# Three-block weight sums of the output projection, made in SBUF from the two-block sums instead of in memory beside the attention heads

## The chip, the cores and the metric

One core of one Trainium2 chip runs the whole program. A time is the device time of one execution in microseconds (us). Where a comparison of two kernels is given, it is of executions on the same chip.

The engines named here are PE (matrix multiply; PEld is its weight load), DVE, ACT and POOL (element-wise work), SP (in this kernel it only issues DMAs), and the core's 16 DMA engines. DMAs are issued by two queues for the most part: SP's (q1 in the profile) and POOL's (q0). Only those of POOL can add what they move to what stands at the destination.

## The reference, cut to what matters

Two layers, each with one input projection, three groups of attention heads, gates, and one output projection, in float32:

```python
h = jnp.einsum('bsd,dn->bsn', x, w_in)            # 512 x 2048 by 2048 x 8278
y_fox = fox_attention(...)                         # 6 heads, 512 keys, forget bias
y_dsa = dsa_attention(...)                         # 6 heads, rotary, 128 selected keys
y_mem = memory_attention(...)                      # 4 heads on 256 memory tokens
y = jnp.concatenate([y_fox, y_dsa, y_mem], axis=-1)   # each times silu(gate)
y = jnp.einsum('bsn,nd->bsd', y, w_out)            # 512 x 2048 by 2048 x 2048
return layer_norm(ALPHA * x + y, ln_gain, ln_bias)
```

## The kernel before

**Precision.** Every float32 product is made of three matrix products: both operands are split into a high and a low part, and high*high, high*low and low*high are added up. The split of a weight tile is one ACT instruction (the high part, `whi`) and one DVE instruction (the low part, `wlo`).

**Stages of a layer.** The index projections; the "values" and "second" stages, in which most columns of the input projection are made; the heads, beside whose steps eight remaining head columns are projected (PE work `c<-...`); and the output projection ("out", PE work `z<-...`). `now[1]` holds the stage's name while the program is written.

**The output projection as seven products.** The 2048 x 2048 product is cut into blocks in the way of Strassen and Winograd, so that seven products of quarter size do the work of eight. `PRODUCTS` names them. Some take sums of weight blocks for their right side: T1 is block (0,0) plus (0,1); T3 is (0,1) plus (1,1); T2, with three blocks, is T1 plus (1,1), or T3 plus (0,0); T4 is T2 plus (1,0). `OUT_ORDER` gives the order, each product for two pairs of column blocks: P1, P1, P7, P7, Q6, Q6, Q4, Q4, Q5, Q5, P2, Q3, P2, Q3. P7 takes T3, Q6 takes T2, Q4 takes T4 and Q5 takes T1.

**Halves.** Each of these 14 steps takes two weight chunks of 1 MB, and each chunk comes in two halves of 512 KB (128 x 1024). A half is 12 matmuls of 512 columns (two row blocks, two 512-column parts, three products). There are 56 halves; they are numbered from 0 here, so that P1 is 0 to 7, P7 8 to 15, Q6 16 to 23, Q4 24 to 31, Q5 32 to 39.

**What is issued beside half n.** The loop at the end of the program does, for each half n: `grow_w(n + 2)`, then `load_w` for the chunk two ahead (half n + 4), then `split_w(n + 3)`, then the matmuls of half n. So a half is loaded four halves ahead and split three ahead. After the last half of a step, `residual` adds the product from PSUM to the tiles `z`, which `load_res` fetched through POOL's queue: two tiles at the start of each of steps 2 to 5 (`RES_LOADS`), four at steps 0 and 1.

**Sums in memory.** `weight_sums` makes a sum of weight blocks in DRAM: first a DMA copies one block (1 MB) into a new DRAM tile `sum`, later a second one adds another block to it. `all_sums` is a generator that is stepped between chunks, and `paced` sets how often: not in the stages "kv" and "second", at each step beside the heads, every third step in "out". Outside "values", `pool_waits` stands ahead of each of these DMAs: a DVE copy `mark` and a POOL instruction `seen` that reads it, so that POOL comes to the DMA no earlier than DVE to that place. Of the output projection's sums there are four of each kind in a layer (two pairs, two chunks): T3, T1 and T2.

**Sums in SBUF.** A chunk of the kind "grown" isn't loaded. `grow_w` adds one more block, by POOL's DMA, to the raw weights of an earlier product, as soon as these have been split; the tile is then the raw weights of the later one. Q4's T4 is grown in this way from Q6's T2. `load_w` puts the weights that another will be grown from into small tiles `grown` (128 x 512 out of the pool `slots`) and all others into tiles `raw` (128 x 1024 out of a pool of seven, which the heads use too).

**Heads.** What a head needs is fetched by SP from memory: transposed columns (`load_turned`, a DMA transpose `vraw<-vt`), values (`vraw<-v`), and for half of them a row of forget sums (`ck<-crow`), from which POOL makes the bias `bt`. POOL also makes the low part of the values, `vl`, which the head's last product `po` on PE takes. All queues are worked off in order: an SP that can't get rid of one DMA holds back all later ones.

Of the kernel before, what the change touches and what calls it, by code (L numbers as in the profile page):

```python
# [102 lines left out]
GROWN = {"Q6": ("P7", (0, 0)), "Q4": ("Q6", (1, 0))}  # L103
# [17 lines left out]
def all_chunks():  # L121

    out = []
    for l in range(DEPTH):
        out += [("mv", l, 0, g) for g in range(4)]
        out += [("mk", l, j, j * HD) for j in range(H_MEM)]
        out += layer_chunks(l)
    return out


def stream():

    wall = all_chunks()
    where = {c: i for i, c in enumerate(wall)}
    out = []

    def product(kind, l, name, pair, gs=(0, 1)):
        right = PRODUCTS[name][2]
        for g in gs:
            at = lambda step: where[kind, l, 2 * pair + step[1], 2 * step[0] + g]  # L140
            if name in GROWN and (kind == "val" or name == "Q4"):
                of, step = GROWN[name]
                src = ("grown", (of, at(step)))
            elif kind == "val" and right in PAIRED and pair >= IN_DRAM:
                src = ("pair", tuple(at(step) for step in PAIRED[right]))
            elif isinstance(right, str):
                src = ("sum", (kind, l, right, pair, g))
            else:
                src = ("wall", at(right))
            out.append(({"val": "vs"}.get(kind, kind), l, (name, pair), g, src))  # L150

    for i, c in enumerate(wall):
        kind, l, j = c[:3]
        if kind == "out":
            if c == ("out", l, 0, 0):
                for name, pair in OUT_ORDER:
                    product("out", l, name, pair)
        elif kind == "val":
            if c == ("val", l, 0, 0):
                for order in (VAL_FIRST, VAL_SECOND):  # L160
                    for pair in range(PAIRS):
                        for name, g in order:
                            product("val", l, name, pair, (g,))
        else:
            out.append((*c, ("wall", i)))
    return out
# [81 lines left out]
def kernel(  # L248
# [26 lines left out]
    def uid(name):  # L275
        count[0] += 1
        return f"{name}_{count[0]}"
# [3 lines left out]
    def slot(name, dt=F32, w=512):  # L281
        t = slots.tile([P, w], dt, tag="s", name=uid(name))
        if name in COUNTED:
            out_now.append(t)
        return t
# [35 lines left out]
    chunks = stream()  # L321
    raw, parts = {}, {}
    sums = {}
# [14 lines left out]
    def half(src, h):  # L338
        return src[:, h * H:(h + 1) * H]

    def load_w(i, pieces=2, some=(0, 1)):
        if i < len(chunks) and chunks[i][4][0] != "grown":
            kind, key = chunks[i][4]
            src = {"wall": lambda: wall[key], "sum": lambda: sums[key],
                   "pair": lambda: wall[key[0]]}[kind]()
            if chunks[i][0] == "out" and chunks[i][2][0] == "Q6":
                for h in some:
                    t = [slot("grown") for _ in range(2)]
                    raw.setdefault(i, []).append(t)
                    for c in range(2):  # L350
                        nc.sync.dma_start(t[c], half(src, h)[:, c * 512:(c + 1) * 512])
                return
            w = DM // pieces
            for c in range(pieces):
                if c * 2 // pieces not in some:
                    continue
                if c * 2 % pieces == 0:
                    raw.setdefault(i, []).append(raws.tile([P, H], F32, tag="raw", name=uid("raw")))
                nc.sync.dma_start(raw[i][-1][:, c * w % H:c * w % H + w], src[:, c * w:(c + 1) * w])
                if i < 3 and c * 2 % pieces == 0:  # L360
                    load_mem(2 * i + c * 2 // pieces)
                if kind == "pair":
                    for e in (2 * c, 2 * c + 1):
                        t = others[i, e] = slot("other")
                        nc.sync.dma_start(t, wall[key[1]][:, e * 512:(e + 1) * 512])
# [93 lines left out]
    def load_mem(j):  # L459
        mem_raw[j] = slot("memraw")  # L460
        eng = nc.scalar if j < 2 and not memT else nc.sync
        eng.dma_start(mem_raw[j], memt_in[:, j * 512:(j + 1) * 512])
# [15 lines left out]
    def split_x(k):  # L478
# [4 lines left out]
        first_sum(k, x)  # L483

    load_w(0, 4, (0,))
    load_w(0, 2, (1,))
    load_w(1, 2)
    load_w(2, 2)
    load_mem(6)
# [33 lines left out]
    def pool_waits():  # L523

        mark, seen = small("mark", 1), small("seen", 1)
        nc.vector.tensor_copy(mark, mhalf)
        nc.gpsimd.tensor_tensor(seen, mark, mhalf, op=ALU.mult)

    SUM_STEPS = {"T1": ((0, 0), (0, 1)), "T3": ((0, 1), (1, 1)), "T2": ("T1", (1, 1)),
                 "T4": ("T2", (1, 0))}  # L530

    def block(kind, l, pair, g, step):
        return wall[where[kind, l, 2 * pair + step[1], 2 * step[0] + g]]

    def add_weights(key, src):
        nc.gpsimd.dma_start(sums[key], src, accum_op=ALU.add, max_dma_last_dim=4 * DM)

    def weight_sums(kind, l, names, pairs, some=(0, 1)):

        for name in names:  # L540
            for n in some:
                step = SUM_STEPS[name][n]
                for pair in pairs:
                    for g in range(2):
                        key = (kind, l, name, pair, g)
                        if isinstance(step, str):
                            src = sums[kind, l, step, pair, g]
                        else:
                            src = block(kind, l, pair, g, step)
                        if now[1] != "values":  # L550
                            pool_waits()
                        if n:
                            add_weights(key, src)
                        else:
                            sums[key] = dram.tile([P, DM], F32, name=uid("sum"))
                            nc.gpsimd.dma_start(sums[key], src)
                        yield

    def paced(gen, steps=PACE):

        n = 0
        for _ in gen:
            n += 1
            while now[1] in ("kv", "second"):
                yield 1
            yield {"heads": 1, "out": 3, "index": 1 + n % 2}.get(now[1], steps)

    def value_sums(l):

        for name in ("T3", "T1"):  # L570
            for n in range(2):
                yield from weight_sums("val", l, (name,), range(IN_DRAM), (n,))

    def all_sums():


        for l in range(DEPTH):
            yield from paced(value_sums(l))
            yield from paced(weight_sums("out", l, ("T3", "T1", "T2"), range(2)))
            while l + 1 < DEPTH and now[0] == l:  # L580
                yield 1

# [10 lines left out]
    now = (0, "index")  # L593
# [932 lines left out]
    for i, (kind, l, j, col, _) in enumerate(chunks):  # L1526
        late = last_half(i)
        if kind == "out":
            step = OUT_ORDER.index(j)
            name, pair = j  # L1530
# [11 lines left out]
        elif kind == "vs":  # L1542
            name, pair = j
# [15 lines left out]
        for h in range(2):  # L1559
            n = 2 * i + h  # L1560
# [83 lines left out]
            if h == 0:  # L1644
                if (kind, j) in HEAD_CHUNKS:
                    if kind == "fq" and j == EARLY:
                        now = (l, "heads")
# [49 lines left out]
        if kind == "mv" and l > 0:  # L1697
            now = (l, "kv")
        if kind == "small":
            now = (l, "index")  # L1700
            stored.clear()
            heads_done.clear()
            memT.clear()
            left.clear()
            if l == 0:
                begin(all_sums(), whole=True)
        if kind == "vs":
            now = (l, "second" if name in ("Q5", "Q3") else "values")
# [13 lines left out]
        if kind == "out" and step == col == 0:  # L1722
            now = (l, "out")
# [4 lines left out]
        if kind == "fq" and j == EARLY:  # L1728
            now = (l, "heads")
# [93 lines left out]
```

## Time and profile before

| what | us |
|---|---|
| median of three runs | 1951.85 (1947.03 to 1957.21) |
| profiled execution | 1972.85 |
| its span, first to last instruction | 1970.8 |
| PE busy in it | 1871.0 (95%) |
| DVE busy | 1599.0 (81%) |
| ACT busy | 1084.7 (55%) |
| POOL busy | 395.0 (20%) |
| head projections `c` of the first layer, start of the first to start of the last | 618.4 to 768.7 |
| the same of the second layer | 1588.3 to 1763.8 |

The profiled execution took 21 us longer than the median of the others; all rows below are from it. Times inside it count from its first instruction. "PEclk" in a row is the share of full clock that PE was granted in the stretch; "DMA" is the mean share that the packets of the 16 DMA engines took, which comes out over 1 where packets of several queues overlap. A row `out<-in` names a written and a read tile. A row that counts instructions may lack a few.

### The profile page before, as it was taken

To read this page: it belongs to the slowest core of one execution; us is meant where nothing else is said; L and a number is where in the kernel's file an instruction comes from. 1 tells how busy PE (TensorE), PEld (TensorE's weight loads), DVE (VectorE), ACT (ScalarE), POOL (GpSimd) and SP (SyncE) were. 2 spreads that over 40 slices of the span, in tenths; PEclk is the share of its full clock that TensorE was granted. 3 is DMA by queue.
4 is the path that set the end of the run, shared out by engine and by line. 5 is a ranking of instruction groups with operands and counts; after the bars stand their busy time and mean duration, and the time that the engine had idled before them with its cause. 6 is when DMAs were issued, how large, how long until landed. Compare 5 with 4: busy or idle time off the path is not lost.

```text
span 1970.8 us, 26414 instructions
## 1 busy us (share of the span) xinstructions
PE 1871.0 (95%) x8930; PEld 1584.2 (80%) x8930; DVE 1599.0 (81%) x2575; ACT 1084.7 (55%) x1666; POOL 395.0 (20%) x571
## 2 busy tenths in 40 slices
PE   9999999999999997899999999999999899748997
PEld 8998888888878876788899888878887788637876
DVE  6789888999777876889968889989886677648798
ACT  5776445555556655655667745445554466337543
POOL 0112111112114131130201122112211042211311
PEclk9999999999999998999999999999999999879999
DMA  9885989889999998596678789998999999996975
GB/s 347 297 261 155 273 248 267 267 270 335 318 342 293 197 238 164 165 275 210 221 264 243 214 273 297 277 282 257 297 354 323 299 269 215 149 114 181 284 218 139
DMA packets 237796, 497.26 MB, mean 252 GB/s; under 512 B 94544, under 2 KB 110928, under 8 KB 232796
## 3 DMA queue, kind: packets, MB, share of 16 engines
q1 hardware_dynamic: 198780, 329.85, 55.8%
q0 software_dynamic: 38304, 164.68, 33.4%
q8 instruction: 70, 1.15, 0.2%
q10 hardware_dynamic: 576, 1.05, 0.1%
q14 instruction: 66, 0.54, 0.1%
HBM read 423.12 MB, written 122.71 MB: 277 GB/s over the span
## 4 chain that ended last, share of the span: by engine, by line
PE 62%; DMA 16%; DVE 10%; issue 6%; ACT 3%; SPq 2%; POOL 1%; DVEq 0%; POOLq 0%; ACTq 0%
PE v L232 33%; PE c L232 14%; PE z L232 8%; DMA other<-in_wall_dram 5%; DMA ck<-crow 3%; DVE wlo L232 3%; DMA vraw<-vt 3%; DMA raw<-in_wall_dram 3%; PE po L232 2%; DVE rope L232 2%; PE ix L232 2%; PE s L232 2%; SPq L1304 1%; DVE z L232 1%; DMA z<-x 1%
## 5 line engine op out<-in xcount | busy, mean ns | idle before, releaser
L232 ACT ACTIVATE whi<-raw 128x1024 fp32r<-128x1024 f32 (+1 forms) x513 | 539.4, 1055 | 469.0 <-PE v L232 240.8
L232 DVE TENSOR_TENSOR wlo<-raw,whi 128x1024 fp32r<-128x1024 f32 (+1 forms) x513 | 626.4, 1227 | 157.3 <-ACT whi L232 154.8
L232 PE MATMUL v<-whi,vxh 128*128 128x512 f32 x768 | 301.6, 393 | 7.9 <-DVE vraw L232 7.9
L232 PE MATMUL v<-wlo,vxh 128*128 128x512 f32 x768 | 300.4, 391 | 2.7 <-DVE wlo L232 2.7
L232 PE MATMUL v<-whi,vxl 128*128 128x512 f32 x768 | 300.2, 391 | 0.0
L232 PE MATMUL v<-whi,xh 128*128 128x512 f32 x576 | 224.2, 389 | 0.0
L232 PE MATMUL v<-whi,xl 128*128 128x512 f32 x576 | 224.1, 389 | 0.0
L232 PE MATMUL v<-wlo,xh 128*128 128x512 f32 x576 | 224.1, 389 | 0.0
L232 PE MATMUL c<-xh,whi 128*128 128x512 f32 (+1 forms) x544 | 202.1, 371 | 0.0
L232 PE MATMUL c<-xh,wlo 128*128 128x512 f32 (+1 forms) x544 | 199.4, 367 | 0.0
L232 PE MATMUL c<-xl,whi 128*128 128x512 f32 (+1 forms) x544 | 199.1, 366 | 0.0
L232 PE MATMUL z<-whi,yl 128*128 128x512 f32 (+1 forms) x434 | 169.9, 392 | 11.2 <-DVE yl L232 11.1
L232 PEld LDWEIGHTS v<-whi,vxh 128*128 128x128 f32 x768 | 145.2, 189 | 40.0 <-issue 10.3
L232 PE MATMUL z<-wlo,yh 128*128 128x512 f32 (+1 forms) x434 | 169.5, 391 | 2.9 <-DVE wlo L232 2.8
L232 PEld LDWEIGHTS v<-wlo,vxh 128*128 128x128 f32 x768 | 145.1, 189 | 33.2 <-DVE wlo L232 3.5
L232 PE MATMUL z<-whi,yh 128*128 128x512 f32 (+1 forms) x434 | 170.1, 392 | 1.4 <-ACT yh L232 1.4
L232 PEld LDWEIGHTS v<-whi,vxl 128*128 128x128 f32 x768 | 144.9, 189 | 30.5
L232 DVE TENSOR_TENSOR raw<-raw,other 128x512 f32<-128x512 f32 x160 | 104.6, 687 | 28.7 <-DMA other<-in_wall_dram 28.2
L232 PEld LDWEIGHTS v<-whi,xl 128*128 128x128 f32 x576 | 108.1, 188 | 22.6
L232 PEld LDWEIGHTS v<-wlo,xh 128*128 128x128 f32 x576 | 108.1, 188 | 22.5
L232 PEld LDWEIGHTS v<-whi,xh 128*128 128x128 f32 x576 | 108.1, 188 | 22.4
L232 PEld LDWEIGHTS c<-xh,wlo 128*128 128x128 f32 x544 | 102.8, 189 | 12.1
(199 smaller groups left out, 3352.5 us busy)
## 6 DMA issues: line engine op xcount, KB each, us to landing
raw<-in_wall_dram SPq DMA_DIRECT2D x371, 512.0 KB, 7.3
other<-in_wall_dram SPq DMA_DIRECT2D x160, 256.0 KB, 9.0
sum<-in_wall_dram POOLq DMA_DIRECT2D x32, 1024.0 KB, 12.1
raw<-in_wall_dram POOLq DMA_DIRECT2D x56, 512.0 KB, 8.2
raw<-sum SPq DMA_DIRECT2D x48, 512.0 KB, 6.0
v<-vraw POOLq DMA_DIRECT2D x72, 256.0 KB, 7.0
vt<-halves POOLq DMA_DIRECT2D x72, 256.0 KB, 6.5
vraw<-v SPq DMA_DIRECT2D x48, 256.0 KB, 5.8
```

The source lines that it names most:

```text
L232: return f(*args, **kw)
L1304: nc.sync.dma_start_transpose(t.bitcast(U16).rearrange("p (a r) -> p a r", a=1), vt_d[j][c])
```

## The change

Three things, and what follows from them:

- `GROWN` is now followed for all products of both kinds. So Q6's T2 is no longer loaded from a sum in memory: it is grown in SBUF out of P7's T3, by adding block (0,0), and Q4's T4 out of it as before. The same tiles serve P7, Q6 and Q4, so the small `grown` tiles are now filled for P7.
- T2 is no longer summed in memory: four copies of 1 MB from `sum` to `sum` and four additions of 1 MB are gone from each layer.
- `paced` doesn't step beside the heads. The four additions that complete T1 now come in "out".

For each layer, 16 DMAs of 256 KB that loaded T2 through SP are gone, and 16 additions of 256 KB through POOL come instead.

```diff
--- before.py
+++ after.py
@@ -138,7 +138,7 @@
         right = PRODUCTS[name][2]
         for g in gs:
             at = lambda step: where[kind, l, 2 * pair + step[1], 2 * step[0] + g]
-            if name in GROWN and (kind == "val" or name == "Q4"):
+            if name in GROWN:
                 of, step = GROWN[name]
                 src = ("grown", (of, at(step)))
             elif kind == "val" and right in PAIRED and pair >= IN_DRAM:
@@ -343,7 +343,7 @@
             kind, key = chunks[i][4]
             src = {"wall": lambda: wall[key], "sum": lambda: sums[key],
                    "pair": lambda: wall[key[0]]}[kind]()
-            if chunks[i][0] == "out" and chunks[i][2][0] == "Q6":
+            if chunks[i][0] == "out" and chunks[i][2][0] == "P7":
                 for h in some:
                     t = [slot("grown") for _ in range(2)]
                     raw.setdefault(i, []).append(t)
@@ -526,8 +526,7 @@
         nc.vector.tensor_copy(mark, mhalf)
         nc.gpsimd.tensor_tensor(seen, mark, mhalf, op=ALU.mult)
 
-    SUM_STEPS = {"T1": ((0, 0), (0, 1)), "T3": ((0, 1), (1, 1)), "T2": ("T1", (1, 1)),
-                 "T4": ("T2", (1, 0))}
+    SUM_STEPS = {"T1": ((0, 0), (0, 1)), "T3": ((0, 1), (1, 1))}
 
     def block(kind, l, pair, g, step):
         return wall[where[kind, l, 2 * pair + step[1], 2 * step[0] + g]]
@@ -543,10 +542,7 @@
                 for pair in pairs:
                     for g in range(2):
                         key = (kind, l, name, pair, g)
-                        if isinstance(step, str):
-                            src = sums[kind, l, step, pair, g]
-                        else:
-                            src = block(kind, l, pair, g, step)
+                        src = block(kind, l, pair, g, step)
                         if now[1] != "values":
                             pool_waits()
                         if n:
@@ -561,9 +557,9 @@
         n = 0
         for _ in gen:
             n += 1
-            while now[1] in ("kv", "second"):
+            while now[1] in ("kv", "second", "heads"):
                 yield 1
-            yield {"heads": 1, "out": 3, "index": 1 + n % 2}.get(now[1], steps)
+            yield {"out": 3, "index": 1 + n % 2}.get(now[1], steps)
 
     def value_sums(l):
 
@@ -576,7 +572,7 @@
 
         for l in range(DEPTH):
             yield from paced(value_sums(l))
-            yield from paced(weight_sums("out", l, ("T3", "T1", "T2"), range(2)))
+            yield from paced(weight_sums("out", l, ("T3", "T1"), range(2)))
             while l + 1 < DEPTH and now[0] == l:
                 yield 1
```

Where POOL's instructions stand is told by the built programs. In the rows below a number behind a name tells one buffer from another, `sum_3669`, `sum_4015`, `sum_4395` and `sum_4798` are the first layer's T1, and `vl` and `bt` belong to the heads.

POOL beside the heads of the first layer, before:

```order
L232 TENSOR_TENSOR seen_6085<-mark_6084,mhalf 128x1
L232 DMA sum_3669<-in_wall_dram 128x2048
L232 TENSOR_TENSOR vl_6082<-vraw_5921,vh_6081 128x512
L232 TENSOR_TENSOR seen_6158<-mark_6157,mhalf 128x1
L232 DMA sum_4015<-in_wall_dram 128x2048
L232 TENSOR_TENSOR vl_6178<-vraw_5944,vh_6177 128x512
L232 TENSOR_TENSOR seen_6285<-mark_6284,mhalf 128x1
L232 DMA sum_4395<-in_wall_dram 128x2048
L232 TENSOR_TENSOR seen_6377<-mark_6376,mhalf 128x1
L232 DMA sum_4798<-in_wall_dram 128x2048
L232 TENSOR_TENSOR seen_6427<-mark_6426,mhalf 128x1
L232 DMA sum_6430<-sum_3669 16x16384
```

And now, from the row ahead of the same `vl_6082`:

```order
L232 AFFINE_SELECT bt_6059<-bt_6059 128x128
L232 TENSOR_TENSOR vl_6082<-vraw_5921,vh_6081 128x512
L232 TENSOR_TENSOR vl_6168<-vraw_5944,vh_6167 128x512
L232 TENSOR_TENSOR vl_6473<-vraw_6207,vh_6472 128x512
L232 TENSOR_SCALAR bt_6556<-ck_6446,cq_1434 128x128
L232 AFFINE_SELECT bt_6556<-bt_6556 128x128
L232 TENSOR_SCALAR bt_6557<-ck_6446,cq_1434 128x256
```

No DMA of a sum, and no `seen`, stands between the heads' instructions any more; the second layer's rows differ in the same way.

POOL at the start of the first layer's output projection, before, ahead of the first growth (`vl_7907` and `vl_7999` are the last two heads' values):

```order
L232 DMA z_7959<-in_x_dram 128x512
L232 DMA z_7961<-in_x_dram 128x512
L232 TENSOR_TENSOR vl_7907<-vraw_7756,vh_7906 128x512
L232 TENSOR_TENSOR vl_7999<-vraw_7763,vh_7998 128x512
L232 DMA z_8076<-in_x_dram 128x512
L232 DMA z_8078<-in_x_dram 128x512
L232 DMA grown_8080<-in_wall_dram 128x512
L232 DMA grown_8081<-in_wall_dram 128x512
```

And now (`vl_7855` and `vl_7970` are those two heads' values; `grown_7754` and the three behind it are of halves 8 and 9):

```order
L232 DMA grown_7754<-in_wall_dram 128x512
L232 DMA grown_7755<-in_wall_dram 128x512
L232 DMA grown_7797<-in_wall_dram 128x512
L232 DMA grown_7798<-in_wall_dram 128x512
L232 TENSOR_TENSOR seen_7910<-mark_7909,mhalf 128x1
L232 DMA sum_3669<-in_wall_dram 128x2048
L232 DMA z_7918<-in_x_dram 128x512
L232 DMA z_7920<-in_x_dram 128x512
L232 DMA grown_7825<-in_wall_dram 128x512
L232 DMA grown_7826<-in_wall_dram 128x512
L232 TENSOR_TENSOR vl_7855<-vraw_7692,vh_7854 128x512
L232 DMA grown_7864<-in_wall_dram 128x512
```

The growth of P7's halves, an addition to T1 and two `z` loads now stand ahead of the values of the last two heads.

POOL later in the same stage, before, at the two `z` loads of step 5 (`z_8340`, `z_8342`):

```order
L232 DMA grown_8149<-in_wall_dram 128x512
L232 DMA grown_8150<-in_wall_dram 128x512
L232 DMA grown_8193<-in_wall_dram 128x512
L232 DMA grown_8194<-in_wall_dram 128x512
L232 DMA grown_8229<-in_wall_dram 128x512
L232 DMA grown_8230<-in_wall_dram 128x512
L232 DMA grown_8254<-in_wall_dram 128x512
L232 DMA grown_8255<-in_wall_dram 128x512
L232 DMA z_8340<-in_x_dram 128x512
L232 DMA z_8342<-in_x_dram 128x512
L232 DMA grown_8282<-in_wall_dram 128x512
L232 DMA grown_8283<-in_wall_dram 128x512
```

And now (`z_8307`, `z_8309`, which the residual behind half 23 takes):

```order
L232 DMA grown_7825<-in_wall_dram 128x512
L232 DMA grown_7826<-in_wall_dram 128x512
L232 DMA grown_7864<-in_wall_dram 128x512
L232 DMA grown_7865<-in_wall_dram 128x512
L232 DMA grown_7924<-in_wall_dram 128x512
L232 DMA grown_7925<-in_wall_dram 128x512
L232 DMA grown_7949<-in_wall_dram 128x512
L232 DMA grown_7950<-in_wall_dram 128x512
L232 TENSOR_TENSOR seen_8299<-mark_8298,mhalf 128x1
L232 DMA sum_4395<-in_wall_dram 128x2048
L232 DMA z_8307<-in_x_dram 128x512
L232 DMA z_8309<-in_x_dram 128x512
```

These two loads stood behind twelve pieces of growth, those of halves 16 to 21; now 28 pieces (halves 8 to 21) and three additions to T1 are ahead of them in the stage.

## The prediction

> **What bounds the kernel now.** The page first. PE is busy nearly all the time, so only places where it stands still can give anything back, and the chain that ended last says what they wait for.
>
> ```profile
> PE 1871.0 (95%) x8930; PEld 1584.2 (80%) x8930; DVE 1599.0 (81%) x2575; ACT 1084.7 (55%) x1666; POOL 395.0 (20%) x571
> PE 62%; DMA 16%; DVE 10%; issue 6%; ACT 3%; SPq 2%; POOL 1%; DVEq 0%; POOLq 0%; ACTq 0%
> ```
>
> Next the table of stretches (length, then busy time and count for PE, PEld, DVE, ACT, POOL; granted clock, DMA share, GB/s). The first two rows run from the first head projection to half 15 of the output projection, in layer 0 and in layer 1; the others are pieces of them.
>
> ```profile
> 618.00:847.00 229.00, 207.09 (x1026) 174.66 (x1025) 180.01 (x354) 138.05 (x298) 60.15 (x89) 0.95 0.92 206
> 1588.00:1841.00 253.00, 206.18 (x1025) 174.10 (x1025) 179.27 (x354) 137.63 (x298) 61.05 (x89) 0.91 0.94 187
> 740.00:760.00 20.00, 12.48 (x58) 10.38 (x58) 10.49 (x17) 6.01 (x11) 4.53 (x9) 0.85 1.18 163
> 760.00:780.00 20.00, 17.40 (x76) 14.93 (x76) 13.16 (x35) 14.66 (x35) 1.44 (x2) 0.76 0.54 131
> 1720.00:1740.00 20.00, 7.00 (x27) 5.54 (x27) 6.96 (x11) 5.25 (x10) 0.00 (x0) 0.67 1.19 73
> 1740.00:1760.00 20.00, 5.66 (x26) 5.30 (x27) 5.63 (x12) 4.71 (x8) 4.53 (x9) 0.56 1.13 206
> ```
>
> The same work takes 229 us in one layer and 253 in the other, with PE idle for 22 and 47 us. In the bad stretches DMA is over-full (1.13 to 1.19) and yet moves little in one of them (73 GB/s). The waits (who waited for whom; us in total, times, longest) in 1690 to 1770, and the last one in 600 to 840:
>
> ```profile
> POOL bt L232 <- DMA ck<-crow: 44.0, 1, 44.0
> PE po L232 <- POOL vl L232: 24.3, 1, 24.3
> PE pt L232 <- ACT bt L232: 9.0, 1, 9.0
> PE po L232 <- POOL vl L232: 8.7, 2, 7.5
> ```
>
> PE waits for `vl`, which stands behind `bt` on POOL, which waits for the row `ck`. Why `ck` is late is seen in time order (start, length, engine):
>
> ```profile
> 1683.30 0.88 POOL L232 DMA_DIRECT2D sum<-in_wall_dram  x1
> ...
> 1690.90 0.82 POOL L232 DMA_DIRECT2D sum<-in_wall_dram  x1
> ...
> 1696.82 0.80 POOL L232 DMA_DIRECT2D sum<-in_wall_dram  x1
> ...
> 1704.38 0.81 POOL L232 DMA_DIRECT2D sum<-in_wall_dram  x1
> 1690.32 42.82 SPq L1304 DMA_TRANSPOSE vraw<-vt  x2
> 1733.24 1.79 SPq L881 DMA_DIRECT2D ck<-crow  x1
> ```
>
> POOL issues the four additions that end T2; two transposes then hold SP for 42.8 us, and `ck` is issued after them. The DMA view of 1683 to 1750 (median us to landing last; queue q0 with packets, MB and share of the 16 engines) and, last line, the landings of `vraw` in 755 to 800, when no sum is under way:
>
> ```profile
> q0 software_dynamic: 576, 4.19, 40.1%
> sum<-in_wall_dram POOLq DMA_DIRECT2D x4, 1024.0 KB, 44.2
> vraw<-vt SPq DMA_TRANSPOSE x5, 25.2
> DMA to landing us min/median/max: 3.4/4.0/7.1
> ```
>
> 4 us for a transpose alone, 25 beside the additions. The Trainium skill ("DMA: Bandwidth & Descriptors", Queues, rings and completion order) says that a DMA engine takes turns among its queues, a whole packet of one, then of the next; the trace agrees in that many small packets of q1 wait behind fewer large ones of q0.
>
> **What the change takes away: the stalls beside the heads.** All twelve DMAs of sums leave that stage in each layer (four additions to T1 are moved, eight DMAs for T2 are gone). I count as theirs: in layer 1 the waits of 24.3 and 9.0 us, in layer 0 that of 8.7. Behind a stall PE runs at half clock for a while: 0.76 granted in 760:780 is 9.6 us at half, less the idle time in it; I take 4.8 us lost in layer 0, and 3.4 in layer 1, where most of the slow clock falls on idle time (0.67 and 0.56 above). Layer 0: 8.7 + 4.8 = 13.5. Layer 1: 24.3 + 9.0 + 3.4 = 36.7. Together 50.2 us. The other idle time up to half 15 (some 13 us a layer: short waits for DVE, the step into "out") stays. `mark` and `seen` cost nothing: POOL is busy 60 of 229 us.
>
> **What it adds: DMA work in "out".** The pace there, and the DMA queues in it: the first line is the end of the stage, the second the stretch from half 6 to half 24 (`z` alone; 18 halves of 12); then 840 to 885, where growth runs, with its queues and issues; then q1 alone in 900 to 960; then q0 in 1624 to 1637, which holds one addition into memory and a few packets.
>
> ```profile
> 900.00:920.00 20.00, 20.00 (x90) 16.54 (x89) 17.27 (x26) 9.86 (x11) 0.00 (x0) 1.00 0.65 216
> 816.00:872.00 56.00, 50.70 (x219) 40.26 (x218) 6.30 (x10) 0.00 (x0) 4.57 (x6) 1.00 0.80 224
> q0 software_dynamic: 2624, 5.24, 57.3%
> q1 hardware_dynamic: 2784, 6.63, 41.5%
> grown<-in_wall_dram POOLq DMA_DIRECT2D x16, 256.0 KB, 11.8
> z<-in_x_dram POOLq DMA_DIRECT2D x4, 256.0 KB, 12.5
> q1 hardware_dynamic: 3421, 12.19, 61.6%
> q0 software_dynamic: 144, 1.05, 44.2%
> ```
>
> 90 matmuls in 20 us are 2.67 us a half. Plain loads cost 61.6% of 60 us for 12.19 MB: 3.03 us per MB, so 0.79 for a tile `z` and 1.59 for a half. In 840 to 885 q0 and q1 add up to 98.8%: the DMA engines are full, and their work adds. q0 took 57.3% of 45 = 25.8 us; less four `z` (3.2) that is 22.6 for 16 pieces of growth, **1.41 us each**. One addition into memory: 44.2% of 13 = **5.75 us**.
>
> Before, the engines had 16 pieces of growth to do there, and PE did not stop. Now the first growth is issued behind half 6, and the `z` tiles of step 5, which the residual behind half 23 takes, stand behind 28 pieces and three sums. Work ahead of them: 28 x 1.41 = 39.5; 3 x 5.75 = 17.3; eight `z` 6.3; P7's last six halves by SP 9.5; together 72.6 us. Time for it: 56 us (second line), and a cushion: splits run three halves ahead, 8.0 us, less one half's split, 1.06 on ACT and 1.23 on DVE (the page's two rows below), so 5.7.
>
> ```profile
> L232 ACT ACTIVATE whi<-raw 128x1024 fp32r<-128x1024 f32 (+1 forms) x513 | 539.4, 1055 | 469.0 <-PE v L232 240.8
> L232 DVE TENSOR_TENSOR wlo<-raw,whi 128x1024 fp32r<-128x1024 f32 (+1 forms) x513 | 626.4, 1227 | 157.3 <-ACT whi L232 154.8
> ```
>
> What is late is 72.6 - 56 - 5.7 = 10.9 us; DVE then waits for `z`, the splits behind it wait, and PE stops. Growth of halves 22 and 23 follows and is late by no more, since the halt gives it time. In layer 1 a broadcast of 1 MB (`out_dram<-in_bias_dram`) stands among them, 3.2 us by the plain price: 14.1. Together **25 us**. Queued behind waiting growth on POOL are the last two heads' `vl` too; their products stand in halves 12 and 14, three halves behind the split that the growth waits for, which hides it. T1's last addition must land before SP, with P2's loads behind, can fetch Q5's last chunk (half 38): 14 halves after it, 37 us, hidden. SP's 16 loads of T2 drop out, which the sum above has already: q1 has nothing to load beside halves 12 to 27. That P7 now lies in `grown` tiles instead of `raw` costs nothing: the same bytes, and the heads' pool is freer.
>
> Both ends of the unknown: if growth and sums cost as plain loads, the work is 22.1 + 9.5 + 6.3 + 9.5 = 47.4 us and nothing is late (no gain beyond: PE had no stop there). If a sum takes what it took in 1683 to 1750, 67 us for four, that is 16.8 each and 33 us more a layer. I take the rows nearest, those of "out" itself: no transposes run there.
>
> By the Trainium skill (same page, Anatomy of one DMA — SWDGE (gpsimd) path) a DMA from POOL takes 2 us and its bytes at 436 GB/s. By that, an estimate: 0.6 us for a piece and 2.4 for a sum, and "out" would hide all. The trace disagrees with it for additions: 1.41 and 5.75.
>
> **Sum.** Against the profiled execution's own 1972.85 us (span 1970.8): - 50.2 + 25 = 1948. That execution took 21.0 us more than the median 1951.85, and layer 1's heads took 24 more than layer 0's. If the others have both layers like layer 0, they lose 27 there: 1951.85 - 27 + 25 = 1950. If the 21 us lie evenly over the program, 1951.85 - 50.2 + 25 = 1927. I take 1936, between: three runs within 10 us speak for one common state of the heads, not for which.
>
> **Rivals.** (B) "Out" hides the new DMA work, by the plain prices or because sums and growth overlap better than their shares add up; for it: PE did not stop with the engines full in 840 to 885; against it: twice the growth. The Trainium skill's fit, cited above, would give this rival. 1951.85 less 27 to 50: 1902 to 1925, say 1913. (C) Slower: sums into memory collide with SP's loads and growth in "out" as they did with the transposes, and the in-order q0 holds `z` and growth behind each. For it: landings of 44 us above; against: those came with transposes. Three sums a layer are ahead of the `z`; at 12.3 us each instead of 5.75 that is 39 us more in both layers: 1975. It decides from about 10 us a sum (25 us more: 1961). (D) An exchange: ordinary runs lose only the 27 us, and "out" takes it back: 1950, no change that can be told.
>
> **Numbers.** Forecast 0.50 (own range 1924 to 1949), B 0.20, C 0.13, D 0.17. A change under 0.5%, 9.8 us, can't be told from none: faster is below 1942.1, slower above 1961.6. Faster: 0.37 of the forecast's, all of B, 0.03 of D: 0.60. Same: 0.13 + 0.12 = 0.25. Slower: C and 0.02 of D: 0.15. Range 1910 to 1964: it leaves out half of B's lower part and most of C.
>
> **What would show it.** Beside the heads: `vraw<-vt` lands in under 8 us at the median, the wait of `bt` for `ck` falls under 10 us, the two long stretches shrink to about 216 us each, and the layers are alike. In "out": DMA full from half 6 to half 31, `z` waiting for its load around half 23, PE idle 8 to 15 us there. Wrong if long waits for transposes stay without sums, or if PE doesn't stop at Q6, or stops for other things than `z` and `grown`.

## The result and the profile after

The changed kernel takes **1929.71 us** at the median (1927.89 to 1930.81, four executions), the kernel before 1954.53 beside it (1947.03 to 1963.89). The ratio is **0.987, 95% interval 0.982 to 0.992**: 24.8 us faster. Twice more, on two chips, the ratio was 0.984 (0.978 to 0.991) and 0.988 (0.985 to 0.992). The profiled execution took 1930.1 us, with a span of 1928.3. A median below counts every execution and a ratio leaves disturbed ones out, so for a kernel whose time varies much the two need not agree to the last per mille.

The page of the changed kernel, busy times and the chain that ended last:

```profile
PE 1861.8 (97%) x8930; PEld 1576.7 (82%) x8930; DVE 1598.3 (83%) x2575; ACT 1086.7 (56%) x1682; POOL 410.1 (21%) x571
PE 66%; DMA 13%; DVE 12%; issue 5%; ACT 3%; SPq 1%; POOL 0%; DVEq 0%; ACTq 0%; POOLq 0%
```

PE does the same 8930 matmuls in 1861.8 us instead of 1871.0, at a granted clock of 0.990 instead of 0.979 over the run, and its share of the chain rises from 62 to 66%, while DMA's falls from 16 to 13.

**Beside the heads.** The table of stretches, again from the first head projection to half 15 in each layer (length, busy time and count of PE, PEld, DVE, ACT, POOL; granted clock, DMA share, GB/s). Below it the landings of `vraw` in 600 to 770, and the one wait of `bt` for `ck` in 600 to 840:

```profile
619.00:830.00 211.00, 201.13 (x1027) 170.55 (x1026) 178.79 (x351) 138.50 (x306) 58.91 (x79) 0.98 0.68 169
1579.00:1790.00 211.00, 200.80 (x1029) 170.71 (x1028) 180.00 (x353) 138.82 (x307) 60.60 (x80) 0.98 0.68 171
```

```profile
DMA to landing us min/median/max: 2.9/3.9/9.4
```

```profile
POOL bt L232 <- DMA ck<-crow: 7.6, 1, 7.6
```

The stretches were 229 and 253 us and are now 211 and 211. PE is idle for 9.9 and 10.2 us of them instead of 21.9 and 46.8, and busy for 201 instead of 206 to 207, at a clock of 0.98 instead of 0.95 and 0.91. No transpose of layer 0 takes longer than 9.4 us.

**In the output projection.** The stretch 840 to 885 of layer 0, its two main queues (packets, MB, share of 16 engines), and the waits that matter in 845 to 885, then in 1795 to 1850 of layer 1:

```profile
840.00:885.00 45.00, 36.08 (x149) 29.28 (x148) 24.74 (x44) 16.91 (x28) 13.03 (x17) 0.89 1.05 246
```

```profile
q0 software_dynamic: 2967, 7.66, 84.2%
q1 hardware_dynamic: 1006, 2.88, 17.4%
```

```profile
DVE z L232 <- DMA z<-in_x_dram: 12.5, 1, 12.5
PE z L232 <- DVE wlo L232: 8.9, 1, 8.9
```

```profile
DVE z L232 <- DMA z<-x: 19.1, 3, 10.9
PE z L232 <- DVE wlo L232: 9.5, 2, 7.6
```

The same halt in time order, on POOL, DVE and PE:

```profile
851.75 1.41 POOL L232 DMA_DIRECT2D sum<-in_wall_dram  x1
854.37 0.59 POOL L232 DMA_DIRECT2D z<-in_x_dram  x1 [1.22 <-PE z L232]
```

```profile
856.47 0.69 DVE L232 TENSOR_TENSOR y<-y,y 128x512 f32<-128x512 f32 x1
869.70 1.50 DVE L232 SCALAR_TENSOR_TENSOR z<-z,z 128x512 f32<-128x512 f32 x2 [12.54 <-DMA z<-in_x_dram]
```

```profile
871.85 0.80 PE L232 MATMUL z<-wlo,yh 128*128 128x512 f32 x1 [8.92 <-DVE wlo L232]
872.44 0.63 PE L232 MATMUL z<-whi,yl 128*128 128x512 f32 x1
```

The engines are over-full (84.2 and 17.4%). The `z` tile is issued at 854.37, behind a sum issued at 851.75, and DVE can take it only at 869.70. DVE stands 12.5 us, the split behind it is late, PE stands 8.9 us, and its matmuls then start 0.43 us apart instead of the 0.22 of full speed (20 us for 90), at half clock.

Before the change PE did not stop there in layer 0 and stopped for 1.4 us in layer 1, though not because `z` was always there. In layer 1, DVE already waited for it (1845 to 1900 of the kernel before):

```profile
DVE z L232 <- DMA z<-x: 10.2, 3, 7.9
```

A wait of 7.9 us cost PE 1.4 us there, and those of 12.5 and 10.9 us cost it 8.9 and 7.6 now: the splits that run ahead cover 3 to 7 us of it.

### The profile page after: what moved, and what is told of

Its sections match the earlier page's. It is cut to its first block, busy times and chain, and to the rows that moved or that the text cites. A ratio compares the mean times of both kernels' runs of the same rounds, so it can differ in the third digit from the quotient of the medians.

```text
span 1928.3 us, 26456 instructions
## 1 busy us (share of the span) xinstructions
PE 1861.8 (97%) x8930; PEld 1576.7 (82%) x8930; DVE 1598.3 (83%) x2575; ACT 1086.7 (56%) x1682; POOL 410.1 (21%) x571
## 3 DMA queue, kind: packets, MB, share of 16 engines
q10 hardware_dynamic: 576, 1.05, 0.1%
## 4 chain that ended last, share of the span: by engine, by line
PE 66%; DMA 13%; DVE 12%; issue 5%; ACT 3%; SPq 1%; POOL 0%; DVEq 0%; ACTq 0%; POOLq 0%
PE v L232 30%; PE c L232 19%; PE z L232 8%; DMA other<-in_wall_dram 5%; DVE wlo L232 5%; DMA raw<-in_wall_dram 3%; DMA z<-x 3%; PE po L232 3%; PE s L232 2%; PE ix L232 2%; DVE raw L232 1%; DMA vraw<-vt 1%; DVE vraw L232 1%; ACT whi L232 1%; PE pt L232 1%
## 5 line engine op out<-in xcount | busy, mean ns | idle before, releaser
L232 ACT ACTIVATE whi<-raw 128x1024 fp32r<-128x1024 f32 (+1 forms) x497 | 523.3, 1056 | 439.3 <-PE v L232 215.9
L232 DVE TENSOR_TENSOR wlo<-raw,whi 128x1024 fp32r<-128x1024 f32 (+1 forms) x497 | 604.3, 1222 | 142.3 <-ACT whi L232 141.4
L232 PEld LDWEIGHTS z<-wlo,yh 128*128 128x128 f32 x434 | 83.5, 192 | 38.2 <-DVE wlo L232 22.0
```

The costliest lines, as they stand in the source:

```text
L232: return f(*args, **kw)
```

## Experiments

Four kernels start from the changed one, four more from the first of these. Where transfers are added, they write memory that nobody reads. A time is a median, the range behind it the lowest and highest execution.

### T1's additions beside the heads again

```diff
-            while now[1] in ("kv", "second", "heads"):
+            while now[1] in ("kv", "second"):
...
-            yield {"out": 3, "index": 1 + n % 2}.get(now[1], steps)
+            yield {"heads": 1, "out": 3, "index": 1 + n % 2}.get(now[1], steps)
```

T2 is still grown. Without buffer numbers, PE and SP have exactly the order of the changed kernel; four POOL transfers a layer move from "out" to the heads.

> The changed kernel with the four additions that end T1 put back beside the heads; T2 is still grown on chip, and no sum is begun in the output projection. Theory (the stalls beside the heads of before came from the eight DMAs of T2, whose additions are issued late in that stage, among the transposes; the additions into T1 come at its start and harm little): the stretch from the first head projection to half 15 stays at 211 to 215 us in both layers, and the stop of 14 us in the output projection is gone, since 3 x 5.75 = 17.3 us of queue work no longer stand ahead of the z tiles of step 5, where 10.9 us were late: 1929.7 - 23.4 = about 1906, with up to 8 us more for the heads. Rival (any addition beside the heads stalls the transposes): that stretch grows by 5 us or more in a layer, vraw lands in over 6 us at the median there, and the time is 1920 to 1930 or above, although the output projection doesn't stop. Second rival (the stop is not made by DMA work ahead of z): the stop at half 28 stays near 14 us.

Measured: **1907.84 us** (1902.27 to 1911.23), ratio to the kernel before 0.976 (0.966 to 0.985). Repeated beside the changed kernel on one chip: 1908.64 against 1930.80, 22.2 us less; ratio to before 0.977 (0.974 to 0.980). Its stretches as above, and T1's additions in 618 to 770 (count, KB each, median us to landing):

```profile
618.00:829.00 211.00, 200.67 (x1029) 170.71 (x1029) 180.13 (x356) 138.29 (x307) 66.96 (x91) 0.98 0.79 191
1565.00:1774.00 209.00, 198.68 (x1025) 168.73 (x1024) 179.06 (x355) 137.32 (x305) 65.56 (x87) 0.99 0.79 197
```

```profile
sum<-in_wall_dram POOLq DMA_DIRECT2D x4, 1024.0 KB, 8.9
vraw<-vt SPq DMA_TRANSPOSE x27, 3.9
```

The heads lose nothing by four additions that land in 8.9 us each; transposes stay at 3.9. The stop in "out" is gone. The table of stretches over that stage in both layers, of the changed kernel and then of this one:

```profile
766.00:953.00 187.00, 171.50 (x770) 141.57 (x770) 150.08 (x243) 99.06 (x167) 45.67 (x55) 0.96 0.86 226
1726.00:1917.00 191.00, 172.29 (x794) 141.76 (x792) 156.99 (x267) 96.44 (x168) 60.53 (x76) 0.97 0.88 225
```

```profile
766.00:940.00 174.00, 168.17 (x769) 139.53 (x768) 148.86 (x239) 98.44 (x164) 39.76 (x47) 0.99 0.80 218
1711.00:1889.00 178.00, 169.70 (x791) 140.14 (x791) 155.38 (x263) 96.53 (x168) 55.44 (x71) 0.99 0.84 219
```

187 and 191 us fall to 174 and 178: 26 us in these two executions, 22 by the medians, which is what moving T1's additions into "out" costs. PE's idle time in them falls from 15.5 and 18.7 us to 5.8 and 8.3. Both kernels move the same bytes; only where four megabytes a layer stand has changed.

### All sums before the heads

```diff
-PACE = 8
+PACE = 5
```

> The changed kernel with its sums begun faster, so that all of a layer's sums, T1's four additions too, end before the heads begin: none beside the heads, none in the output projection. Theory (a sum costs PE time only beside transposes or ahead of the z tiles in the output projection): heads 211 us a layer as after the change, no stop of more than 4 us in the output projection, about 1906. Rival (the sums' DMA work has no slack in the projections before the heads either): PE waits there for other or raw some 10 to 25 us more, and the time stays within 10 us of 1930.

Measured: 1911.48 us (1909.49 to 1916.18), ratio 0.977 (0.970 to 0.985). The theory's direction holds, with a time 5 us above its 1906. PE's waits in the projections before layer 1's heads, 1085 to 1574, show a part of it:

```profile
PE v L232 <- DVE wlo L232: 8.4, 3, 4.1
```

With T1 beside the heads the same row, in 1083 to 1565, is

```profile
PE v L232 <- DVE wlo L232: 4.0, 3, 1.4
```

DMA work isn't free there either, but it costs a few us and not twenty.

### z by SP's queue

```diff
-        nc.gpsimd.dma_start(z[st, dc], src[st * P:(st + 1) * P, dc * 512:(dc + 1) * 512])
+        nc.sync.dma_start(z[st, dc], src[st * P:(st + 1) * P, dc * 512:(dc + 1) * 512])
```

> The changed kernel with one edit: the z tiles of the output projection are loaded by SP's queue instead of POOL's, so they no longer stand behind growth and additions in one queue; the DMA work is the same. Theory (two things are late by about 11 us, first z by its place in the queue and then the growth by the sheer work of full DMA engines): the wait of DVE for z (12.5 and 19.1 us) is gone, part of it comes back as waits of the splits for grown or of SP's other loads, PE stops for 3 to 8 us a layer instead of 12: 1912 to 1922. Rival (only the order in POOL's queue makes the stop): no stop above 4 us, about 1906. Rival (only the sheer work): the stop stays at 11 to 14 us with grown as what is waited for, about 1930.

Measured: **1914.01 us** (1910.70 to 1915.31), ratio 0.978 (0.970 to 0.986). The waits for `z` are gone, and in 845 to 885 and 1795 to 1850 splits wait for growth instead:

```profile
ACT whi L232 <- DMA grown<-in_wall_dram: 9.0, 4, 6.0
```

```profile
ACT whi L232 <- DMA grown<-in_wall_dram: 10.3, 6, 5.5
```

So 15.7 us of the stop belong to the place of `z` in POOL's queue, and some 6 (1914.01 - 1907.84) are not taken away by moving `z`; the splits' waits for growth point to the work of the engines. The time is that of the first theory.

### The eight transfers of T2 beside the heads of the changed kernel

```diff
+            begin(spare_sums(l), whole=True)
...
+                    pool_waits()
+                    if n:
+                        nc.gpsimd.dma_start(spare[key], src, accum_op=ALU.add, max_dma_last_dim=4 * DM)
+                    else:
+                        spare[key] = dram.tile([P, DM], F32, name=uid("spare"))
+                        nc.gpsimd.dma_start(spare[key], src)
```

> The changed kernel plus eight DMAs of sums a layer beside the heads, as before the change: four copies and four additions of 1 MB each, issued behind the same waits, into memory that nobody reads. They add no dependence and move nothing else. Theory (the stalls beside the heads of before are these transfers against the transposes): vraw lands in 6 us or more at the median there, the wait of bt for ck grows to 20 us or more, the stretch from the first head projection to half 15 grows from 211 us to 229 to 253, the time is 1948 to 1990. Rival (the stalls of before came from what T1's additions and T2's readers do to the order, not from the transfers): the stretch stays below 218 us and the time within 8 us of 1930.

Measured: **1961.03 us** at the median of ten (1938.64 to 1967.15, and one of 3101.44), against 1929.71 without them: 31 us. The transfers stand somewhat earlier than T2's did: the additions are issued from 666 to 688 in layer 0, T2's were from 713 to 736. The ten executions do not agree as those of the changed kernel do, and the profiled one, at 1939.67 us, is one of the two lowest. Its rows for the two stretches and, in 600 to 785, its transposes:

```profile
619.00:840.00 221.00, 203.96 (x1026) 172.27 (x1025) 181.13 (x359) 138.89 (x306) 69.09 (x95) 0.97 0.86 199
1589.00:1799.00 210.00, 199.25 (x1025) 168.95 (x1024) 180.53 (x359) 137.19 (x305) 67.78 (x94) 0.99 0.86 209
```

```profile
vraw<-vt SPq DMA_TRANSPOSE x31, 4.8
```

Layer 0 lost 10 us, layer 1 none. The transfers cost the time that the theory said, at the median; the expected size of each sign (6 us or more for a transpose, 229 to 253 us a stretch) is not in this milder execution.

### The same transfers at their old places

From here on the kernel with T1 beside the heads (1907.84 us) is the base. T2's eight transfers follow T1's, from their old sources; orders of PE and SP are those of the base.

```diff
             yield from paced(weight_sums("out", l, ("T3", "T1"), range(2)))
+            yield from paced(spare_sums(l))
```

> The kernel with T1's additions beside the heads and T2 grown (1907.84 us), plus the eight transfers that made T2 before, at their old places and from their old sources: four copies of T1 into other memory and four additions to them, which nobody reads. It differs from that kernel by these eight transfers alone, and from the kernel before only in how the output projection gets T2. Theory (these eight cause the stalls of before, and nothing else of the change moves the time): 1945 to 1970, like the kernel before, with a spread of more than 15 us; vraw lands in 5 us or more at the median in the heads and in over 25 us at worst. Rival (T2's loads from memory in the output projection cost a part of what was lost): within 10 us of 1908.

Measured: **1943.53 us** (1935.98 to 1976.66), and 1941.47 (1929.66 to 1975.54) on another chip, beside 1957.02 and 1951.94 of the kernel before. Eight transfers that nobody waits for cost 33 to 36 us. The theory said 1945 to 1970 and that nothing else of the change moves the time; both medians lie below that. Stretches, then waits in 600 to 840:

```profile
618.00:851.00 233.00, 205.45 (x1027) 173.91 (x1026) 180.32 (x364) 138.23 (x307) 73.74 (x106) 0.94 0.93 208
1585.00:1811.00 226.00, 206.22 (x1027) 174.38 (x1027) 179.86 (x364) 137.86 (x305) 74.69 (x104) 0.95 0.98 219
```

```profile
POOL bt L232 <- DMA ck<-crow: 39.5, 3, 24.7
PE po L232 <- POOL vl L232: 17.0, 2, 16.0
```

This is the picture of the kernel before: 233 and 226 us, and the same chain from `ck` to `vl` to PE. The ratio to before, 0.994 both times (0.990 to 0.998; 0.991 to 0.997), leaves some 11 us that these eight transfers do not explain. What they are was not tried. What is left between the two kernels is how "out" gets T2, read from memory by SP or grown, but the profiled executions show little of it there: from half 16 to the last product "out" takes 109 us in layer 0 of both, and 116 against 113 in layer 1.

### Copies in the place of the late additions

```diff
-                        nc.gpsimd.dma_start(spare[key], block("out", l, pair, g, (1, 1)),
-                                            accum_op=ALU.add, max_dma_last_dim=4 * DM)
+                        nc.gpsimd.dma_start(spare[key], block("out", l, pair, g, (1, 1)))
```

> The same with one edit: the four late transfers are plain copies of the same blocks over the same memory instead of additions. Bytes written and places are the same; an addition costs 5.75 us of all engines per MB and a copy some 3. Theory (the additions hold the engines and the transposes wait for their packets): most of the loss is gone, 1908 to 1925. Rival (any MB of large packets in POOL's queue does it to the transposes): the same time as with the additions, 1945 or more.

Measured: **1925.11 us** (1920.45 to 1928.81), at the border of the theory's range: of the 36 us, 18 go and 17 stay, so half of the loss is gone and not most of it. The stretch 720 to 738 has three of the four late transfers in both kernels. First with additions: the stretch and its queues (packets, MB, share of 16 engines).

```profile
720.00:738.00 18.00, 18.00 (x88) 15.08 (x88) 16.73 (x37) 11.00 (x28) 2.84 (x4) 1.00 1.17 172
```

```profile
q0 software_dynamic: 293, 2.15, 61.8%
q1 hardware_dynamic: 1798, 0.93, 54.4%
```

Then with copies:

```profile
720.00:738.00 18.00, 18.00 (x89) 15.07 (x88) 16.78 (x38) 9.89 (x25) 3.44 (x7) 1.00 1.03 340
```

```profile
q1 hardware_dynamic: 3248, 2.98, 59.2%
q0 software_dynamic: 89, 3.15, 44.1%
```

With additions the full engines move 172 GB/s, with copies 340. q0 takes 5.2 us of all engines per MB (0.618 x 18 / 2.15) against 2.5 (0.441 x 18 / 3.15), and q1's own packets get dearer: 0.54 against 0.33 us of all engines per 100 of them (0.544 x 18 / 1798; 0.592 x 18 / 3248). The edit also changed the size of q0's packets, 7 KB with additions and 35 KB with copies; whether the adding or the number of packets makes the difference is open. Copies are not harmless either: in layer 1, two transposes issued at 1616.7 and 1625.1 landed after 23.5 and 23.3 us, beside T1's last addition and the first two copies, all of which took 18 to 20 us.

### ck by ACT's queue

```diff
-        nc.sync.dma_start(cks[h], bass.AP(tensor=crow_d[l].tensor, offset=crow_d[l].offset + h * SEQ,
+        nc.scalar.dma_start(cks[h], bass.AP(tensor=crow_d[l].tensor, offset=crow_d[l].offset + h * SEQ,
```

> The kernel with all twelve transfers beside the heads (additions, not copies), and one edit: the row ck is fetched by ACT's queue instead of SP's, so it no longer stands behind a transpose that holds SP. Theory (PE stops because ck is issued late and bt, vl behind it): the wait of bt for ck falls under 12 us and half or more of the loss is gone, 1910 to 1935. Rival (the late transposes stop the heads by themselves, through vraw): within 10 us of the kernel with the twelve transfers and ck by SP.

Measured: 1960.70 us (1944.54 to 2017.20). The waits of `bt` for `ck` fell as the theory said (600 to 785, then 1560 to 1750):

```profile
POOL bt L232 <- DMA ck<-crow: 6.8, 3, 5.2
```

```profile
POOL bt L232 <- DMA ck<-crow: 9.1, 2, 8.3
```

The time did not; it rose by 17 us. The planner had charged ACT for the new instruction and set the work of every engine in another order, so this run decides nothing on the time. One `ck` in it landed after 21.8 us although no transpose stands in ACT's queue. The experiment was repeated with the order kept:

```diff
-        nc.scalar.dma_start(cks[h], bass.AP(tensor=crow_d[l].tensor, offset=crow_d[l].offset + h * SEQ,
+        tc.nc.scalar.dma_start(cks[h], bass.AP(tensor=crow_d[l].tensor, offset=crow_d[l].offset + h * SEQ,
```

> The kernel with all twelve transfers beside the heads, ck fetched by ACT's queue, and now every other instruction of every engine in exactly the order that it has with ck on SP; the first try with ACT let the order of all engines change. Theory (half or more of the loss comes by ck, issued late behind a transpose that holds SP, and bt and vl behind it): the waits of bt for ck fall from 39.5 and 19.7 us to under 10, PE's stops of 16 and 5 us ahead of a product with vl are gone, and of the 36 us lost against the kernel with T1's additions alone 15 to 30 come back: 1915 to 1930. Rival (vraw is late by itself): the same waits turn up at vraw and the time stays within 6 us of the kernel with the twelve transfers.

> The kernel with the twelve transfers and ck by SP again, on the chip of the run above: 1938 to 1955, with a spread of more than 10 us.

Measured: **1937.38 us** (1922.55 to 1959.19) against 1941.47 with `ck` by SP, 4 us less where the theory had 15 to 30. By the ratios to the kernel before it is 7 us (0.990 and 0.994, with intervals that overlap), so a small gain can't be excluded. The profiled execution, at 1959.19 us, is the slowest of the ten; its rows show a bad stall and not a usual one. Waits in 600 to 785 of the run with ACT's queue; the issue of one `ck`; SP in the same time; and the landings of `ck` in that stretch:

```profile
POOL bt L232 <- DMA ck<-crow: 45.6, 3, 29.7
PE po L232 <- POOL vl L232: 24.7, 2, 21.0
```

```profile
727.17 0.33 ACTq L895 DMA_DIRECT2D ck<-crow  x1
```

```profile
722.19 34.95 SPq L1318 DMA_TRANSPOSE vraw<-vt  x2
```

```profile
DMA to landing us min/median/max: 4.3/6.9/37.2
```

ACT issues `ck` at 727.17 without delay, while SP is held for 35 us by transposes, and `ck` is late all the same: this one landed after 37.2 us. Here the row is late without standing behind a transpose, while the engines are taken. The rival's own reason is not what shows either: in layer 0 PE still waits by `bt` and `vl`. The DMA view of the worst stretch, 738 to 764 of this run:

```profile
DMA packets 934, 2.67 MB, mean 103 GB/s; under 512 B 533, under 2 KB 533, under 8 KB 653
q0 software_dynamic: 305, 2.29, 71.9%
q1 hardware_dynamic: 493, 0.12, 18.7%
q10 hardware_dynamic: 134, 0.25, 3.8%
```

The additions take 71.9% of the engines for 2.29 MB, 8.2 us per MB (0.719 x 26 / 2.29), where the prediction had measured 5.75 for one whole addition (1.05 MB) alone.

### The changed kernel and the best one again

> The changed kernel once more, so that it stands beside the others on one chip. 1927 to 1933 as at first, with a spread of a few us; the kernel before, whose time depends on how the stalls beside the heads fall, should spread over more than 15 us again.

> The kernel with T1's additions beside the heads and T2 grown again, now beside the changed kernel on one chip: 1903 to 1912; 20 us or 1.0% below the changed kernel.

> The changed kernel on the same chip as the run above: 1926 to 1931.

Measured: 1927.05 us (1926.80 to 1929.25) on one chip, 1930.80 (1926.16 to 1935.84) on another, where the kernel with T1 beside the heads took 1908.64 (1902.66 to 1909.77). The kernel before had 1957.02 (1923.49 to 1971.90) and 1951.94 (1937.79 to 1981.69). The kernel with T1 beside the heads beats both.

## Why the prediction was right

Forecast were 1936 us and "faster" at 0.60; measured 1929.71. The forecast's own case came true in both halves: the stalls beside the heads went, and "out" stops for `z`. The sizes and the cause of the stalls need a closer look.

**The heads, forecast 50.2 us.** In the profiled executions the stretches give back 18 + 42 = 60 us. The idle time fell by 12.0 and 36.6 us, 48.6, where the waits taken were 42.0; the rest of the idle time, set at some 13 us a layer that would stay, fell to 10. The busy time fell by 6.0 and 5.4 us, 11.3 together, where the slow clock was set at 8.2. The signs named for it are there: transposes at 3.9 us, a wait for `ck` of 7.6, both layers alike, and 211 us a stretch where 216 was said.

**The step of it that failed** is "`ck` is issued after them". The trace of before did show that order, and taking the sums away does end the wait, but the place in SP's queue is not what costs most of the time: with `ck` on ACT's queue, in an otherwise unchanged order, 4 to 7 of some 35 us come back, and in the profiled execution `ck` is as late. And "all twelve" is too many: T1's four cost nothing at the heads' start (1907.84 us), T2's eight cost 33 to 36. The loss comes with T2's transfers in flight among back-to-back transposes. With copies in place of the late additions half of it stays; whether the adding or the size of the packets makes the other half was not separated. That small transfers are late while the engines are full stands; by which rule was not shown. The Trainium skill ("DMA: Bandwidth & Descriptors", Queues, rings and completion order) has an engine drain a whole packet of one queue before the next. The rows count six packets of q1 for one of q0 with additions and 36 with copies, and they don't show which of them are one packet in its sense, so they neither confirm nor refute it.

**"Out", forecast 25 us** (10.9 and 14.1). From half 16 to its last product the stage takes 120.4 and 124.7 us, before the change 108.5 and 115.8: 21 us more. It is 26 us longer than with T1 beside the heads, 13 and 13, of which PE is idle for 9.7 and 10.4 (8 to 15 were said) and the rest is slow clock; the time of the kernels differs by 22. That the stop needs T1's three additions ahead of `z` is shown: growth alone, in that kernel, leaves none. The wait is `z` for its load, in both layers, with DMA over-full, as the sum of the work ahead of it (72.6 us) had it. PE's stop falls a few halves later than the late `z`, since the splits run ahead: the cushion of 5.7 us. The claim that growth is late by no more than `z` holds only in part: with `z` on another queue 6 us stay. The bias broadcast, 3.2 us more in layer 1, is not seen.

**The sum, and luck in it.** For the profiled execution the prediction's sum gave 1948 us, and the profiled execution after took 1930.1: the heads gave 10 us more than said, "out" took 4 less, and some 3 lie elsewhere. For the ordinary execution three readings stood: 1950 if both layers lost 27 us as in layer 0, 1927 if the profile's surplus of 21 us lay evenly, 1936 between. 1927 came nearest. But the common state of the heads that "three runs within 10 us" were to speak for isn't there: the kernel before lay between 1923 and 1987 us in all but one of its executions. By the medians on one chip, the kernel that has neither stall is 1951.94 - 1908.64 = 43 us faster than the kernel before, and the change gives back 22 of it. These are 43 and 22 where the sum had 50 and 25, and the 43 hold some 11 us that the prediction had no term for. The two errors nearly cancel, and 1936 was a choice between two readings, so that it lies 6 us from the result is in part luck.

**The rivals.** (B) "Out" hides the new work: no, it is 21 to 26 us longer. The Trainium skill's fit ("DMA: Bandwidth & Descriptors", Anatomy of one DMA — SWDGE (gpsimd) path) would have it hidden; the measured time disagrees, as the prediction's own rows for additions did. (C) Sums in "out" collide as with the transposes: no; the stage loses 13 us a layer, not the 32 of that case. (D) An exchange: no, since the heads lost more than 27 us; T2's transfers alone bring back 33 to 36.

**What the change is, then**: two moves in one. T2 grown on chip, with its sums in memory gone, gains 45 to 48 us (by the ratios 0.977 and 0.976); T1 moved to "out" loses 22 of them. Of the first, 33 to 36 are shown by putting T2's transfers back, and some 11 are open.

## What to carry to other kernels

Transfers that nobody waits for can be the costliest in a stage: look at what else is in flight beside them, and compare GB/s at full DMA share (172 against 340 here) before asking who waits for whom. When a change moves work out of a bad place, add up the queue of the place that receives it, first of all what stands in order ahead of a small load that is needed soon. A wait in the chain names the transfer that came last, not the reason: give that transfer its own queue, in an unchanged order, before its queue is blamed. And see where the profiled execution lies among the others before its rows are taken for the rule.

## What the runs showed that was not expected

Four additions of 1 MB beside the heads cost nothing and land in 8.9 us; with eight more behind them, in the worst stretch of the run with `ck` by ACT, the additions take 8.2 us of all engines per MB, and the core moves 103 GB/s with the engines some 95% busy. The Trainium skill ("Advanced Engine Details and Errata", X-Bar Transpose (TRN2)) calls such transposes as fast as ordinary transfers; the traces agree without late additions (3.9 us at the median in the changed kernel for `vraw<-vt`, and for as large a plain load `vraw<-v`). Beside late additions both are slow, as 715 to 756 of the kernel with T2's transfers at their old places shows, where plain loads of 512 KB, 5.7 us in the changed kernel, take about as long as the transposes:

```profile
raw<-in_wall_dram SPq DMA_DIRECT2D x4, 512.0 KB, 23.3
vraw<-vt SPq DMA_TRANSPOSE x5, 17.8
```

The size of such a stall changes from one execution to the next: the kernel before lay between 1923 and 1987 us in all but one of its executions, the changed kernel between 1926 and 1936. A single profile shows one draw of it. So the 253 us of layer 1 and the 229 of layer 0, in one execution, need be no property of the layers: with T2's transfers put back it was 226 and 233.
